# One tail load of a log-sum-exp kernel, issued as three transfers with uneven shares for the DMA engines

## The chip, the cores and the metric

The kernel runs on one core of one Trainium2 chip. The metric is the device time of one execution in microseconds (us). The median of three runs of the kernel before is 161.57 us; the three lie between 161.51 and 161.59 us. A profile was taken of one more execution. All views, line numbers and durations below come from that execution.

## The reference

The input `x` is a float32 array of 32 x 512 x 1024. For every row of 1024 numbers the reference gives the logarithm of the sum of exponentials, in its stable form:

```
max_x = np.max(x, axis=-1, keepdims=True)
max_x.squeeze(-1) + np.log(np.sum(np.exp(x - max_x), axis=-1))
```

There are 16384 such rows, so 67.11 MB are read and 0.07 MB are written.

## The kernel before, in words

**The layout.** The 16384 rows are spread over 128 partitions, 128 rows of the input to each. One such row in every partition is called a column here: 128 columns of 1024 numbers (`d`). The kernel does not subtract the maximum first. It takes the exponential and the sum directly, then tests whether all sums lie in a safe range (L276 to L294, with a small TensorE product that adds up over the partitions), and only if they do not, it computes everything again with the maximum subtracted (L302 to L345). With this input that branch is not taken.

**The loads.** `LOADS` (L22 to L28) lists 19 loads. Its first number is the load's size in columns: the first has 15.625 columns, then they shrink, the fifteenth (index 14) has 0.75 columns and the last (index 18) 0.46875. A load is one DMA of all 128 partitions (L139), so it moves one run of bytes to each partition: 3072 bytes for the fifteenth. All loads are issued in order on SyncE's queue (SP). They land in a ring of 48 columns per partition (`ring`), and `load` waits (L136) until the work that used the same place of the ring is done. Each load has a semaphore of its own, `landed[i]`, that stands at 16 when the whole load has landed.

**The work on a load.** ScalarE (ACT) waits for `landed[i]` (L186) and takes the exponential in place (L227). Then the letters of the load's plan say how the sums over the columns are made: `R` is one VectorE (DVE) reduction (L238), `G` lets GpSimd (POOL) add the two halves first (L233) and DVE reduce what is left (L157), `T` lets DVE add the two halves of one column with the sum as a by-product (L165). Loads 9 to 16 (counted from 0) have `T` columns, 16 adds with the one of load 17. Load 17 (`a`) holds the first part of the last column and is summed by DVE; load 18 (`b`) holds its last 480 numbers, which ACT exponentiates and sums itself (L222).

**The end.** `HELD` is 15: before the add of load 15, DVE also waits until load 16 has landed (L244, L245). An early store of 112 finished columns is issued on SP after load 18 (L261). When DVE's adds are done, ACT takes the logarithm of the last 16 columns (L265, then L267, which needs ACT's own sum of load 18), copies that sum (L270), and SP issues the last store (L272). Beside that DVE makes the range test's two sums (L276, L280), PE adds them up in three products (L286, L288, L290; the third one needs the copy of L270), DVE compares (L294), and ACT and DVE read the answer and branch (L297, L302). SP ends the program when both stores have landed.

**Names that the prediction uses.** A load is called by its index: load 14 is the fifteenth. `done_before` is the position of a load in the input, `here` its position in the ring.

Of the kernel before, what the change touches and what calls it, by code (L numbers as in the profile page):

```python
# [11 lines left out]
B = 16  # L12

HELD = 15

# [36 lines left out]
def kernel(  # L54
# [5 lines left out]
    nc = tc.nc  # L60
# [4 lines left out]
    P = nc.NUM_PARTITIONS  # L65
# [19 lines left out]
    def source(e0, size):  # L85
        assert e0 >= W * d or e0 + size <= W * d
        return x_rest[:, e0 - W * d : e0 - W * d + size] if e0 >= W * d else x_rows[:, e0 : e0 + size]
# [9 lines left out]
    def sbuf(name, cols, dtype=fp32, rows=P):  # L97
        return nc.alloc_sbuf_tensor(name, [rows, cols], dtype).ap()

    ring = sbuf("ring", RING * d)  # L100
# [14 lines left out]
    landed = [nc.alloc_semaphore(f"landed{i}") for i in range(len(loads))]  # L115
    act = Counted(nc, nc.scalar, "act")
# [16 lines left out]
    def load(i, here, done_before, size):  # L133
        for a, b, who, at in users:
            if a < here + size and b > here:
                sp.wait(who, at)  # L136
        assert not any(p0 < here + size and p0 + s * d > here for _, p0, s, _ in folded)
        users[:] = [u for u in users if not (u[0] < here + size and u[1] > here)]
        return nc.sync.dma_start(  # L139
            out=ring[:, here : here + size], in_=source(done_before, size)  # L140
        ).then_inc(landed[i], 16)

    c = 0
    p = 0
    here = 0
    done_before = 0
# [6 lines left out]
    def sum_folded():  # L153
        for c0, p0, s, at in folded:
            dve.wait(pool, at)
            half = ring[:, p0 : p0 + s * d].rearrange("p (c d) -> p c d", d=d)[:, :, 0:H]
            at = dve.did(nc.vector.reduce_sum(out=sumexp[:, c0 : c0 + s], in_=half, axis=AX.X))  # L157
            users.append((p0, p0 + s * d, dve, at))
            summed.append((c0, c0 + s, at))
        folded.clear()  # L160

    def add_halves(v, col):
        h = v.shape[-1] // 2
        lo = v[:, 0:h]
        return dve.did(nc.vector.scalar_tensor_tensor(  # L165
            out=lo, in0=lo, scalar=1.0, in1=v[:, h : 2 * h],
            op0=ALU.mult, op1=ALU.add, accum_out=sumexp[:, col : col + 1],
        ))

    def check_early(c):  # L170
        dve.wait(act, summed_by_act)
        dve.wait(dve, dve.n)
        for op, col in ((ALU.min, LEAST), (ALU.add, TOTAL)):
            dve.did(nc.vector.tensor_reduce(  # L174
                out=sumexp[:, col : col + 1], in_=sumexp[:, 0:c], op=op, axis=AX.X
            ))

    for i, (size, parts) in enumerate(loads):
        if here + size > RING * d:
            assert here == p  # L180
            p = here = 0
        dma = load(i, here, done_before, size)
        first_load = first_load or dma.ins
        end = here + size
        done_before += size
        act.wait(landed[i], 16)  # L186
        for k, part in enumerate(parts):
            if part[0][0] == "H":
                sum_folded()
                continue  # L190
            if part[0][0] == "C":
                assert not folded
                checked = c
                check_early(c)
                continue
            if part[0][0] == "L":
                assert c >= W
                assert dve.seen[act.sem.num] >= summed_by_act
                act.wait(dve, max(at for c0, _, at in summed if c0 < W))
                ln_early = act.did(nc.scalar.activation(  # L200
                    out=res[:, 0:W], in_=sumexp[:, 0:W], func=AF.Ln
                ))
                continue
            if part[0][0] == "A":
                assert here == p
                for _ in range(part[0][1]):
                    v = ring[:, p : p + d]
                    summed_by_act = act.did(nc.scalar.activation(
                        out=v, in_=v, func=AF.Exp, accum_out=sumexp[:, c : c + 1]
                    ))  # L210
                    users.append((p, p + d, act, summed_by_act))
                    by_act += 1
                    c += 1
                    p += d
                    here += d
                continue
            rows = sum(s for how, s in part if how in "RTG")
            more = any(q[0][0] not in "HLC" for q in parts[k + 1 :])
            upto = p + rows * d if more else end
            v = ring[:, here:upto]  # L220
            if part[-1][0] == "b":
                last = act.did(nc.scalar.activation(  # L222
                    out=v, in_=v, func=AF.Exp, accum_out=rest
                ))
                here = upto
                continue
            at = act.did(nc.scalar.activation(out=v, in_=v, func=AF.Exp))  # L227
            here = upto
            for how, s in part:
                rows = ring[:, p : p + s * d].rearrange("p (c d) -> p c d", d=d)  # L230
                if how == "G":
                    pool.wait(act, at)
                    folded.append((c, p, s, pool.did(nc.gpsimd.tensor_tensor(  # L233
                        out=rows[:, :, 0:H], in0=rows[:, :, 0:H], in1=rows[:, :, H:d], op=ALU.add,
                    ))))
                elif how == "R":
                    dve.wait(act, at)
                    users.append((p, p + s * d, dve, dve.did(nc.vector.reduce_sum(  # L238
                        out=sumexp[:, c : c + s], in_=rows, axis=AX.X
                    ))))  # L240
                    summed.append((c, c + s, dve.n))
                elif how == "T":
                    if i == HELD:
                        nc.vector.wait_ge(landed[i + 1], 16)  # L244
                        nc.vector.nop(nofuse=True)  # L245
                    dve.wait(act, at)
                    for r in range(s):
                        n_sums = add_halves(rows[:, r, :], c + r)
                        users.append((p + r * d, p + (r + 1) * d, dve, n_sums))
                        summed.append((c + r, c + r + 1, n_sums))  # L250
                elif how == "a":
                    dve.wait(act, at)
                    summed.append((LAST, NC, add_halves(ring[:, p:upto], LAST)))
                    s = 0
                c += s
                p += s * d
        assert here == end
# [10 lines left out]
        out=res[:, LAST:NC], in_=rest, func=AF.Ln, bias=sumexp[:, LAST:NC]  # L268
# [8 lines left out]
        out=clamped[:, 0 : LEAST + 1 - checked], in0=sumexp[:, checked : LEAST + 1], scalar=LOW,  # L277
# [3 lines left out]
        out=total, in_=sumexp[:, checked : TOTAL + 1], axis=AX.X  # L281
# [20 lines left out]
    with nc.If(all_fine < 1):  # L302
# [5 lines left out]
        for c0 in range(0, NC, RING):  # L308
# [6 lines left out]
            for c1, c2 in ((c0, edge), (edge, c0 + s)):  # L315
                if c1 == c2:
                    continue
                nc.scalar.dma_start(
                    out=ring[:, (c1 - c0) * d : (c2 - c0) * d],
                    in_=source(c1 * d, (c2 - c1) * d),  # L320
# [4 lines left out]
                out=neg, in_=v, op=ALU.max, axis=AX.X, negate=True  # L325
# [3 lines left out]
                out=v, in0=v, in1=neg[:, :, None].to_broadcast([P, s, d])  # L329
# [5 lines left out]
                out=sumexp[:, c0 : c0 + s], in_=v, axis=AX.X  # L335
# [70 lines left out]
```

## Time and profile before

| What | Value |
|---|---|
| median of 3 runs | 161.57 us (161.51 to 161.59) |
| the profiled execution's own time | 161.52 us |
| its span, first to last instruction | 160.2 us |
| DVE busy | 116.2 us (73%) |
| ACT busy | 114.6 us (72%) |
| POOL busy | 33.3 us (21%) |
| PE busy | 0.4 us |
| bytes moved by DMA | 67.18 MB, mean 419 GB/s over the span |

The span is 1.3 us shorter than the execution's own time; what lies around it is not in the trace. An engine's busy time is a mean over stages with different limits: early in the run ACT waits for loads, at the end the engines work back to back. The rows of a timeline give the start, the duration, the engine and line, the operation and the shapes. Instructions of one engine overlap by some hundredths of a microsecond, so a start may lie a little ahead of the end of the instruction before. The rows on DMA issues give a transfer's size and the time from its issue to its landing, so issue plus that time is the landing.

### The profile page before, as it was taken

The numbers are of one execution on the slowest core, as the hardware profiler recorded it, in microseconds if no ns is written. First come the engines' busy times: TensorE is split into PE (matmuls) and PEld (weight loads), VectorE is DVE, ScalarE is ACT, GpSimd is POOL, SyncE is SP. The second block draws the span as 40 slices with busy tenths as digits, with TensorE's granted clock in tenths as the row PEclk, the third lists the DMA queues.
The fourth block names the chain that finished last, engine by engine and source line by source line (L and its number), as shares of the span: only waits on it lengthen the run. The fifth ranks groups of instructions, "written<-read, shape, count | busy, mean of one in ns | idle before, by whom it ended". The sixth has DMA issues, their size and how long they took to land.

```text
span 160.2 us, 183 instructions
## 1 busy us (share of the span) xinstructions
PE 0.4 (0%) x6; PEld 0.3 (0%) x6; DVE 116.2 (73%) x56; ACT 114.6 (72%) x32; POOL 33.3 (21%) x14
## 2 busy tenths in 40 slices
PE   0000000000000000000000000000000000000001
PEld 0000000000000000000000000000000000000000
DVE  0000000029997599999999699929999999999996
ACT  3000069970999429992799349965998999899996
POOL 0000000000000000000000000980580589996000
DMA  8998999699599699996999999997999999999993
GB/s 272 495 511 368 400 514 482 289 514 513 256 512 512 272 479 478 478 463 268 453 467 467 467 430 430 430 430 332 499 395 448 437 417 389 443 412 423 417 409 105
DMA packets 3025, 67.18 MB, mean 419 GB/s; under 512 B 592, under 2 KB 720, under 8 KB 1488
## 3 DMA queue, kind: packets, MB, share of 16 engines
q1 hardware_dynamic: 3024, 67.18, 97.9%
q14 instruction: 1, 0.01, 0.0%
HBM read 67.11 MB, written 0.07 MB: 419 GB/s over the span
## 4 chain that ended last, share of the span: by engine, by line
DMA 53%; DVE 21%; ACT 19%; POOL 5%; issue 0%; PE 0%; SPq 0%
DMA ring<-in_x_dram 53%; ACT ring L227 19%; DVE sumexp L238 15%; POOL ring L233 5%; DVE ring L165 3%; DVE sumexp L157 2%; SPq L139 0%; DVE clamped L276 0%; PE count L286 0%; ACT res L200 0%; DVE fine L294 0%; PE count L290 0%; PE count L288 0%
## 5 line engine op out<-in xcount | busy, mean ns | idle before, releaser
L227 ACT ACTIVATE ring<-ring 128x16000 f32<-128x16000 f32 (+24 forms) x25 | 112.2, 4546 | 42.7 <-DMA ring<-in_x_dram 42.7
L238 DVE TENSOR_REDUCE sumexp<-ring 128x9 f32<-128x9216 f32 (+7 forms) x10 | 89.8, 8999 | 39.1 <-ACT ring L227 39.1
L233 POOL TENSOR_TENSOR ring<-ring 128x2048 f32<-128x2048 f32 (+5 forms) x8 | 33.0, 4133 | 112.2 <-ACT ring L227 112.1
L157 DVE TENSOR_REDUCE sumexp<-ring 128x4 f32<-128x2048 f32 (+5 forms) x8 | 16.5, 2079 | 3.4 <-POOL ring L233 3.4
L165 DVE SCALAR_TENSOR_TENSOR ring<-ring 128x512 f32<-128x512 f32 (+1 forms) x16 | 9.8, 672 | 0.1
L126 ACT ACT_TABLE_LOAD x1 | 1.3, 1283 | 1.4 <-PEq L63 1.4
L165 DVE DVE_READ_ACCUMULATOR ring<-ring 128x1 f32 x16 | 1.3, 83 | 0.0
L222 ACT ACTIVATE ring<-ring 128x480 f32<-128x480 f32 x1 | 0.6, 603 | 0.0
L286 PE MATMUL count<-far,bad 128*1 128x1 f32 x2 | 0.2, 164 | 158.6 <-DVE clamped L276 158.6
L174 DVE TENSOR_REDUCE sumexp<-sumexp 128x1 f32<-128x106 f32 x2 | 0.4, 258 | 0.0
L294 DVE TENSOR_SCALAR fine<-count 1x1 int32<-1x1 f32 x1 | 0.1, 147 | 0.4 <-PE count L290 0.4
L286 PEld LDWEIGHTS count<-far,bad 128*1 128x1 f32 x2 | 0.1, 80 | 158.6 <-DVE clamped L276 158.6
L127 POOL MEMSET ones<- 128x1 f32 x1 | 0.1, 98 | 1.0 <-POOLq L63 1.0
L200 ACT ACTIVATE res<-sumexp 128x112 f32<-128x112 f32 x1 | 0.3, 279 | 0.0
L267 ACT ACTIVATE res<-rest,sumexp 128x1 f32<-128x1 f32 x1 | 0.2, 244 | 0.0
L265 ACT ACTIVATE res<-sumexp 128x15 f32<-128x15 f32 x1 | 0.2, 216 | 0.0
L276 DVE SCALAR_TENSOR_TENSOR clamped<-sumexp 128x23 f32<-128x23 f32 x1 | 0.2, 183 | 0.0
L288 PE MATMUL count<-total,ones 128*1 128x1 f32 x2 | 0.2, 164 | 0.0
L290 PE MATMUL count<-sumexp,ones 128*1 128x1 f32 x2 | 0.2, 164 | 0.0
L280 DVE TENSOR_REDUCE total<-sumexp 128x1 f32<-128x24 f32 x1 | 0.2, 175 | 0.0
L222 ACT ACTIVATION_READ_ACCUMULATOR ring<-ring 128x1 f32 x1 | 0.2, 153 | 0.0
L270 ACT COPY sumexp<-rest 128x1 f32<-128x1 f32 x1 | 0.1, 150 | 0.0
(8 smaller groups left out, 0.8 us busy)
## 6 DMA issues: line engine op xcount, KB each, us to landing
ring<-in_x_dram SPq DMA_DIRECT2D x1, 8048.0 KB, 38.8
ring<-in_x_dram SPq DMA_DIRECT2D x1, 8016.0 KB, 57.4
ring<-in_x_dram SPq DMA_DIRECT2D x1, 8000.0 KB, 21.3
ring<-in_x_dram SPq DMA_DIRECT2D x1, 7472.0 KB, 25.8
ring<-in_x_dram SPq DMA_DIRECT2D x1, 7312.0 KB, 23.0
ring<-in_x_dram SPq DMA_DIRECT2D x1, 6720.0 KB, 21.6
ring<-in_x_dram SPq DMA_DIRECT2D x1, 5200.0 KB, 17.6
ring<-in_x_dram SPq DMA_DIRECT2D x1, 3584.0 KB, 19.1
```

The lines of the kernel that those rows point to most:

```text
L126: nc.scalar.preload_act_table_set("natural_log_exp_and_others")
L157: at = dve.did(nc.vector.reduce_sum(out=sumexp[:, c0 : c0 + s], in_=half, axis=AX.X))
L165: return dve.did(nc.vector.scalar_tensor_tensor(out=lo, in0=lo, scalar=1.0, in1=v[:, h : 2 * h], op0=ALU.mult, op1=ALU.add, accum_out=sume ...
L174: dve.did(nc.vector.tensor_reduce(out=sumexp[:, col : col + 1], in_=sumexp[:, 0:c], op=op, axis=AX.X))
L200: ln_early = act.did(nc.scalar.activation(out=res[:, 0:W], in_=sumexp[:, 0:W], func=AF.Ln))
L222: last = act.did(nc.scalar.activation(out=v, in_=v, func=AF.Exp, accum_out=rest))
L227: at = act.did(nc.scalar.activation(out=v, in_=v, func=AF.Exp))
L233: folded.append((c, p, s, pool.did(nc.gpsimd.tensor_tensor(out=rows[:, :, 0:H], in0=rows[:, :, 0:H], in1=rows[:, :, H:d], op=ALU.add,))))
L238: users.append((p, p + s * d, dve, dve.did(nc.vector.reduce_sum(out=sumexp[:, c : c + s], in_=rows, axis=AX.X))))
L265: act.did(nc.scalar.activation(out=res[:, W:LAST], in_=sumexp[:, W:LAST], func=AF.Ln))
L267: ln_last = act.did(nc.scalar.activation(out=res[:, LAST:NC], in_=rest, func=AF.Ln, bias=sumexp[:, LAST:NC]))
L286: pe.did(nc.tensor.matmul(count, lhsT=bad, rhs=far, start=True, stop=False))
```

## The change

The fifteenth load, index 14, is issued as three transfers: partitions 0 to 111, 112 to 119 and 120 to 127. Each moves the same columns as before, 3072 bytes for each partition, from the same place in the input to the same place in the ring. All three count on the semaphore of load 14, and ACT waits for 48 on it instead of 16. The other 18 loads are issued as before. The words that describe the change say that the lower eight DMA engines then move nine of this load's packets and the other eight engines seven.

```diff
+UNEVEN = 14
+SHARES = (0, 112, 120, 128)
...
-        return nc.sync.dma_start(
-            out=ring[:, here : here + size], in_=source(done_before, size)
-        ).then_inc(landed[i], 16)
+        shares = SHARES if i == UNEVEN else (0, P)
+        for p0, p1 in zip(shares, shares[1:]):
+            dma = nc.sync.dma_start(
+                out=ring[p0:p1, here : here + size], in_=source(done_before, size)[p0:p1]
+            ).then_inc(landed[i], 16)
+        return dma
...
-        act.wait(landed[i], 16)
+        act.wait(landed[i], 16 * (len(SHARES) - 1) if i == UNEVEN else 16)
```

## The prediction, made before the changed kernel ran

> **What bounds the kernel now.** I read the page first, for the totals, and then the chain of waits in order of time, for the stage that the change touches.
>
> ```profile
> span 160.2 us, 183 instructions
> q1 hardware_dynamic: 3024, 67.18, 97.9%
> DMA 53%; DVE 21%; ACT 19%; POOL 5%; issue 0%; PE 0%; SPq 0%
> ```
>
> The DMA engines have work for 97.9% of the span, and the chain that ended last is DMA for 53% of it. Load 14 comes in the last 8 us, so that share says little about it. The chain's last pieces do:
>
> ```profile
> 119.57 23.79 DMA ring<-in_x_dram
> 143.36 0.02 issue
> 143.38 6.75 ACT ring L227 x2
> 150.13 0.18 ACT res L200
> 150.32 3.74 ACT ring L227 x2
> 154.06 0.02 issue
> 154.09 2.36 DVE ring L165 x7
> 156.44 0.15 issue
> 156.60 1.74 DVE ring L165 x7
> 158.33 0.02 issue
> ```
>
> The last transfer on the chain is load 9, which lands at 119.57 + 23.79 = 143.36. From there ACT works through its exponentials, and from 154.09 DVE's adds follow one another. No later load is on the chain. The question is how much room loads 14 to 18 have, so I put landings beside the starts of ACT. The timeline of SP gives the issues of loads 14 to 18, and the DMA view their sizes and times to landing:
>
> ```profile
> 132.86 0.43 SPq L139 DMA_DIRECT2D ring<-in_x_dram  x1
> 133.33 0.47 SPq L139 DMA_DIRECT2D ring<-in_x_dram  x1
> 133.84 0.45 SPq L139 DMA_DIRECT2D ring<-in_x_dram  x1
> 134.33 4.72 SPq L139 DMA_DIRECT2D ring<-in_x_dram  x1
> 139.10 3.74 SPq L139 DMA_DIRECT2D ring<-in_x_dram  x1
> ring<-in_x_dram SPq DMA_DIRECT2D x1, 384.0 KB, 21.9
> ring<-in_x_dram SPq DMA_DIRECT2D x1, 336.0 KB, 22.3
> ring<-in_x_dram SPq DMA_DIRECT2D x1, 320.0 KB, 22.6
> ring<-in_x_dram SPq DMA_DIRECT2D x1, 272.0 KB, 22.7
> ring<-in_x_dram SPq DMA_DIRECT2D x1, 240.0 KB, 18.6
> ```
>
> ACT's timeline gives when each of them was taken up and when the logarithm begins; the last row is SP's and is the store behind it:
>
> ```profile
> 155.12 0.83 ACT L227 ACTIVATE ring<-ring 128x768 f32<-128x768 f32 x1
> 155.85 0.75 ACT L227 ACTIVATE ring<-ring 128x672 f32<-128x672 f32 x1
> 156.51 0.72 ACT L227 ACTIVATE ring<-ring 128x640 f32<-128x640 f32 x1
> 157.13 0.64 ACT L227 ACTIVATE ring<-ring 128x544 f32<-128x544 f32 x1
> 157.72 0.60 ACT L222 ACTIVATE ring<-ring 128x480 f32<-128x480 f32 x1
> 158.35 0.22 ACT L265 ACTIVATE res<-sumexp 128x15 f32<-128x15 f32 x1
> 158.75 0.34 SPq L272 DMA_DIRECT2D out_dram<-res  x1
> ```
>
> Issue plus time to landing: load 14 lands at 132.86 + 21.9 = 154.8 and is taken up at 155.12; load 15 at 155.6 for 155.85; load 16 at 156.4 for 156.51; load 17 at 157.0 for 157.13; load 18 at 139.10 + 18.6 = 157.70 for 157.72. The **room** shrinks from 0.36 us to 0.02. For load 18 ACT itself would have been ready a little earlier: neighbours overlap by 0.09 us (156.51 + 0.72 - 157.13 = 0.10, 155.85 + 0.75 - 156.51 = 0.09), so after 157.13 + 0.64 = 157.77 it could have begun at 157.68. Load 18 holds ACT up by 0.04 us and no other late load holds it at all.
>
> **What an earlier landing can give.** Of these 0.04 us nothing need arrive: L265 begins at 158.35, just behind the end of DVE's last add in the chain (158.33), and DVE's adds do not hang on load 18. So an earlier landing of loads 14 to 18 gives between 0 and 0.04 us; I take 0, because the chain ends in DVE.
>
> **What a later landing costs.** A delay D of loads 14 to 18 is eaten by the room of loads 14 to 16 as long as D is under some 0.1, but at load 18 it arrives almost whole: L222 starts D later, and with it L267, the copy L270 (which the last PE product waits for) and the store L272. So the cost is about D.
>
> **The change part by part.** The price of one packet comes first. Between the landings of loads 9 (143.36) and 18 (157.70) lie loads 10 to 18. Four more sizes complete the list:
>
> ```profile
> ring<-in_x_dram SPq DMA_DIRECT2D x1, 1584.0 KB, 24.8
> ring<-in_x_dram SPq DMA_DIRECT2D x1, 1232.0 KB, 27.4
> ring<-in_x_dram SPq DMA_DIRECT2D x1, 896.0 KB, 20.2
> ring<-in_x_dram SPq DMA_DIRECT2D x1, 640.0 KB, 21.4
> ```
>
> They sum to 4352 KB, with loads 14 to 18 (1552 KB) to 5904 KB, in 14.34 us: 412 KB/us, 25.7 KB/us for one of 16 engines. A packet of load 14 is 384 / 128 = 3 KB and takes its engine 3 / 25.7 = **0.117 us**. Eight packets to each engine become nine for half of the engines and seven for the other half: half of the engines reach load 15 0.117 us later, half 0.117 us earlier, and since all later packets queue behind, this shift stays until load 18.
>
> Two more completions fall on the engines that serve the small transfers. No row shows one alone. Load 18 takes 157.70 - 157.03 = 0.67 us after load 17, and its 240 / 16 = 15 KB an engine need 15 / 25.7 = 0.58, so all that is fixed in a load (eight packets and one completion) is at most 0.09 us, and one ninth of it 0.01. Two completions cost between 0 and 0.18 us; I take 0.02, the ninth twice, because packets follow each other without a gap. A lower engine is then 0.117 + 0.02 = 0.14 us later, an upper one 0.117 earlier.
>
> **Which engines end last** decides the sign. The table by stretches shows the engines running out of packets behind load 18 (the last column but one is the DMA share; the small early store, 56 KB, still fills in):
>
> ```profile
> 157.10:157.20 0.10, 0.00 (x0) 0.00 (x0) 0.10 (x1) 0.10 (x2) 0.00 (x0) 1.00 0.89 267
> 157.20:157.30 0.10, 0.00 (x0) 0.00 (x0) 0.10 (x3) 0.10 (x2) 0.00 (x0) 1.00 0.43 128
> 157.30:157.40 0.10, 0.00 (x0) 0.00 (x0) 0.10 (x3) 0.10 (x1) 0.00 (x0) 1.00 0.23 58
> 157.40:157.50 0.10, 0.00 (x0) 0.00 (x0) 0.10 (x1) 0.10 (x1) 0.00 (x0) 1.00 0.12 31
> 157.50:157.60 0.10, 0.00 (x0) 0.00 (x0) 0.10 (x1) 0.10 (x1) 0.00 (x0) 1.00 0.01 0
> ```
>
> 0.89 x 16 = 14 engines are busy, then 7, 4, 2 and none: the engines end over some 0.4 us, and two of them trail by about 0.1 us, one packet's time. No view names them. If both are upper engines, loads 15 to 18 land up to 0.12 us earlier, worth 0. If one or both are lower engines, loads land 0.14 later, worth +0.14 us. By mere counting both are upper in (8/16) x (7/15), about a quarter; so I take **+0.14**. The Trainium skill, "DMA: Bandwidth & Descriptors", section "Latency and other measured facts", says that DMA engines 7 and 15 are usually slower in traces, with a cause that it ties to transfers issued by GpSimd. Two trailing engines fit its count; one of that pair would be a lower engine, which also gives +0.14, while without such a pair the sum stays open between 0 and +0.14.
>
> **The issues.** SP issues two transfers more, 2 x 0.45 = 0.9 us. Loads 15 to 18 queue behind them, and so does the early store. The issues of loads 17 and 18 already last 4.72 and 3.74 us; nothing shown ends them, so SP seems to wait for room in the DMA queue. Load 18's issue is over at 142.84, its data moves in the last 0.7 us ahead of 157.70. Even if two more transfers ahead of it cost two loads' waiting, until load 11 has landed (1232 KB above, issued in the row below), it would be issued 7 us early:
>
> ```profile
> 122.72 0.44 SPq L139 DMA_DIRECT2D ring<-in_x_dram  x1
> ```
>
> 122.72 + 27.4 = 150.1. That cover hides the 0.9 us entirely; the cost is 0. No wait instruction is added; ACT's wait counts to 48 instead of 16, at no cost.
>
> **Sum.** 161.52 (the profiled execution: a span of 160.2 and 1.3 around it) + 0.14 = 161.66. That execution lies 0.05 below the median of the runs, so the forecast is **161.71 us**, +0.09%. Its own range, packets at their usual pace, is 161.50 to 161.85: the 0.04 gain below, both completions a little dearer above.
>
> **Rival 1, slower: the small transfers share a way into SBUF.** Every transfer in this trace spreads over all 128 partitions, so no row shows eight engines writing to eight neighbouring partitions. 25.7 KB/us an engine may be the pace of the engine or of the place it writes to. If each place serves 8 of 128 partitions, with neighbours together, the eight packets of a small transfer queue at one, two or four places. I take two, between one and four. There four packets follow each other: 4 x 0.117 = 0.47 us a transfer, 0.94 for both, and a lower engine needs 7 + 8 = 15 packet times instead of 8, D = 0.82. If the late engines are upper ones, some 0.2 of this falls into the spread. That gives +0.6 to +0.82: 162.2 to 162.4, middle 162.3. At one place D is (7 + 16 - 8) x 0.117 = 1.76 (163.3), at four 3 x 0.117 = 0.35 (161.9). The transfer of 112 may suffer too, since seven partitions an engine no longer match places of eight; twice its 7 x 0.117 would add up to 0.82. It decides from D = 0.32, three packet times. For it speaks that 16 equal paces fit either reading; against it that a burst of two packets an engine, 6 KB, may be absorbed on the way, and that the profile has no sign of such a queue. The Trainium skill, "SBUF — State Buffer", section "Door 1: The DMA port swizzle", states such a mapping: four neighbouring partitions lie on one port, and it gives 27.6 GB/s to partitions 0 to 3 against 104 to 0 to 15. By that rule partitions 112 to 119 reach two ports, the case of 162.3; no trace here shows it.
>
> **Rival 2: both trailing engines are upper ones**, and landings come earlier. It gives 161.53 to 161.57 for the reason above. Being within the noise it counts with the forecast.
>
> **Rival 3: the change does not do what it says.** If the small transfers spread over all engines, nothing shifts: 161.57. If one engine takes all eight packets, it has 7 + 16 instead of 8: +1.76, 163.3.
>
> **A real gain** of over 0.32 us would need ACT to begin earlier than at 143.38, which load 14 can't bring, or a large idle time behind load 14, which the rows do not have.
>
> **How the numbers follow.** 0.2% is 0.32 us, about what a measurement can tell from no change. Packets at their usual pace (with rival 2): 0.52, all of it within 0.2%. Sharing: 0.40, of which 0.38 slower and 0.02, the mildest, within 0.2%. Rival 3: 0.04, half within, half slower. Unforeseen: 0.04, half faster, half slower. So same is 0.52 + 0.02 + 0.02 = 0.56, slower 0.38 + 0.02 + 0.02 = 0.42, faster 0.02. The range reaches from 161.50 to 162.80; the harder sharing above it and a single engine are left out, at about 0.15. The likeliest case alone has 161.50 to 161.85.
>
> **What would show it.** Right: after load 14 the times to landing of loads 14 to 18 move by at most 0.15 us, L222 starts between 157.7 and 157.9, and a transfer of 8 partitions takes no longer than others. Rival 1: the DMA share drops below 0.9 in the stretch where load 14 moves, load 18 lands at 158.3 or later, ACT shows an idle gap ahead of L227's 128x768, or of the ones behind it. Rival 3: the landing moves by 0 or by over 1.5 us. The forecast is wrong if ACT waits for load 14 at all.

## The result, and the profile after

The changed kernel takes 162.14 us (median of 6 runs, 162.04 to 162.71), the kernel before beside it 161.51 us (6 runs, 161.49 to 161.59). The ratio is 1.0043, with a 95% interval from 1.0033 to 1.0054: **slower by 0.63 us**. The profiled execution of the changed kernel took 162.08 us, with a span of 160.7.

The same three lines of the page, after the change:

```profile
span 160.7 us, 185 instructions
q1 hardware_dynamic: 3040, 67.18, 97.8%
DMA 51%; DVE 31%; ACT 11%; POOL 4%; SPq 1%; issue 0%; PE 0%
```

The two new instructions are SP's issues, and the packets grew by 16: they are small ones, for the bytes are the same 67.18 MB. Nothing on the page says where 0.63 us went; the chain does. Its pieces from the issue of load 13 on, after the change (start, duration, what; the short `issue` pieces and what follows the last row are left out):

```profile
132.60 0.43 SPq L145
133.08 0.45 SPq L145
133.58 0.44 SPq L145
134.06 21.48 DMA ring<-in_x_dram
155.56 0.85 ACT ring L234
156.44 0.58 DVE ring L172
157.06 1.77 DVE ring L172 x7
158.85 0.20 DVE clamped L283 x2
```

Before, the last transfer on the chain was load 9. Now it is the third part of load 14, issued at 134.06 and landed at 155.54, where all of load 14 had landed at 154.8 before. ACT's timeline (L234 is the former L227, L229 the former L222) shows the wait in brackets, and how the late loads are taken up; below it the issue and landing of load 18:

```profile
155.56 0.84 ACT L234 ACTIVATE ring<-ring 128x768 f32<-128x768 f32 x1 [0.20 <-DMA ring<-in_x_dram]
157.67 0.66 ACT L234 ACTIVATE ring<-ring 128x544 f32<-128x544 f32 x1
158.31 0.60 ACT L229 ACTIVATE ring<-ring 128x480 f32<-128x480 f32 x1
138.79 4.08 SPq L145 DMA_DIRECT2D ring<-in_x_dram  x1
ring<-in_x_dram SPq DMA_DIRECT2D x1, 240.0 KB, 19.5
```

ACT stands idle for 0.20 us ahead of load 14, and load 18 lands at 138.79 + 19.5 = 158.29 instead of 157.70. L229 begins 158.31 - 157.72 = 0.59 us later than before. The other late path is the one on the chain: DVE waits for the exponential of load 14 and starts its add 0.46 us later than before (156.44 instead of 155.98):

```profile
156.44 0.69 DVE L172 SCALAR_TENSOR_TENSOR ring<-ring 128x512 f32<-128x512 f32 x1 [0.28 <-ACT ring L234]
155.98 0.69 DVE L165 SCALAR_TENSOR_TENSOR ring<-ring 128x512 f32<-128x512 f32 x1
```

The first row is after the change, the second before. From there DVE's adds follow one another, and the range test begins at 158.85 instead of 158.36, 0.49 later. The two paths meet in the last product on PE, which starts 0.55 us later than before (159.37 instead of 158.82). All loads from 14 on land late, and that is the loss. The issues are not it: load 18's is over at 138.79 + 4.08 = 142.87, against 142.84 before.

The view that shows the cause is the table by stretches, of 0.6 us each. The last two columns are the share of time for which the DMA engines had a packet in hand, and the GB/s that they moved. Before:

```profile
153.60:154.20 0.60, 0.00 (x0) 0.00 (x0) 0.54 (x3) 0.60 (x2) 0.00 (x0) 1.00 1.02 408
154.20:154.80 0.60, 0.00 (x0) 0.00 (x0) 0.60 (x3) 0.60 (x1) 0.00 (x0) 1.00 1.03 413
154.80:155.40 0.60, 0.00 (x0) 0.00 (x0) 0.60 (x3) 0.60 (x2) 0.00 (x0) 1.00 1.05 418
```

After:

```profile
153.60:154.20 0.60, 0.00 (x0) 0.00 (x0) 0.59 (x2) 0.60 (x2) 0.00 (x0) 1.00 1.02 360
154.20:154.80 0.60, 0.00 (x0) 0.00 (x0) 0.57 (x1) 0.60 (x1) 0.00 (x0) 1.00 1.11 244
154.80:155.40 0.60, 0.00 (x0) 0.00 (x0) 0.60 (x3) 0.56 (x1) 0.00 (x0) 1.00 0.98 320
155.40:156.00 0.60, 0.00 (x0) 0.00 (x0) 0.60 (x3) 0.44 (x1) 0.00 (x0) 1.00 1.03 405
```

The engines are as busy as before, but they move 244 GB/s where they moved 413. A packet takes longer, no engine is out of work. The trace's records of single packets say it directly: before, every packet of load 15 (2688 bytes) took 0.107 us; after the change they took 0.158 on average and up to 0.233, and those of load 14 (3072 bytes) 0.128 on average instead of 0.121. So most of the loss falls on the load behind the split one. The missing bytes are (48 + 169 + 98) GB/s x 0.6 us = 189 KB, which at 410 GB/s is 0.46 us of all engines. A full DMA share is no sign of a full rate; the column beside it must be read too.

### The profile page after: what moved, and what is told of

Read it like the earlier page. It is cut to its first block, busy times and chain, and to the rows that moved or that the text cites. A ratio compares the mean times of both kernels' runs of the same rounds, so it can differ in the third digit from the quotient of the medians.

```text
span 160.7 us, 185 instructions
## 1 busy us (share of the span) xinstructions
PE 0.5 (0%) x6; PEld 0.3 (0%) x6; DVE 116.2 (72%) x56; ACT 114.8 (71%) x32; POOL 33.3 (21%) x14
## 2 busy tenths in 40 slices
DMA packets 3041, 67.18 MB, mean 418 GB/s; under 512 B 608, under 2 KB 736, under 8 KB 1504
## 3 DMA queue, kind: packets, MB, share of 16 engines
q1 hardware_dynamic: 3040, 67.18, 97.8%
## 4 chain that ended last, share of the span: by engine, by line
DMA 51%; DVE 31%; ACT 11%; POOL 4%; SPq 1%; issue 0%; PE 0%
DMA ring<-in_x_dram 51%; DVE sumexp L245 27%; ACT ring L234 11%; POOL ring L240 4%; DVE sumexp L164 2%; DVE ring L172 1%; SPq L145 1%; DVE clamped L283 0%; PE count L297 0%; PE count L293 0%; DVE fine L301 0%; PE count L295 0%; SPq L54 0%
## 5 line engine op out<-in xcount | busy, mean ns | idle before, releaser
L234 ACT ACTIVATE ring<-ring 128x16000 f32<-128x16000 f32 (+24 forms) x25 | 112.4, 4548 | 43.1 <-DMA ring<-in_x_dram 43.1
L229 ACT ACTIVATE ring<-ring 128x480 f32<-128x480 f32 x1 | 0.6, 602 | 0.0
L229 ACT ACTIVATION_READ_ACCUMULATOR ring<-ring 128x1 f32 x1 | 0.2, 154 | 0.0
```

Of the source, the lines that this page charges most:

```text
L229: last = act.did(nc.scalar.activation(out=v, in_=v, func=AF.Exp, accum_out=rest))
```

## The experiments

**The theory** after this reading: the packets of load 14 meet on the way into SBUF, because neighbouring partitions are served at a common place (rival 1 of the prediction, called the sharing theory in the expectations). The 0.59 us that the expectations start from is the delay of load 18's landing. **The rivals**: a fixed price for each transfer; the uneven shares themselves; neighbouring input rows that meet in HBM. The diffs below are extracts: counts on semaphores and the allocation of new tiles are left out.

### Three transfers by columns

Load 14 is cut by columns instead of partitions:

```diff
+        cuts = (0, size // 3, 2 * size // 3, size) if i == 14 else (0, size)
+        for c0, c1 in zip(cuts, cuts[1:]):
+            dma = nc.sync.dma_start(
+                out=ring[:, here + c0 : here + c1], in_=source(done_before + c0, c1 - c0)
+            ).then_inc(landed[i], 16)
```

> Load 14 as three transfers of all 128 partitions, 256 columns each (1 KB a packet); every engine gets the same. Sharing theory (eight neighbouring partitions queue at few places in SBUF): all partitions are spread, so load 18 lands within 0.1 us of before (157.70) and the time is 161.5 to 161.6. Rival, a fixed price for each transfer (0.59 us for the change's two more transfers, 0.3 each): load 18 lands near 158.3, time near 162.1.

Measured: 161.58 us against 161.58, ratio 1.0002 (0.9992 to 1.0011). Every packet of loads 15 to 18 took as long in the trace as before. Two more transfers, with their issues and with completions on every engine, cost nothing that can be measured here. The fixed price falls.

### No uneven shares

```diff
-SHARES = (0, 112, 120, 128)
+SHARES = (0, 112, 128)
```

> Load 14 as two transfers, 112 and 16 partitions, eight packets to every engine, so no uneven shares. Sharing theory: sixteen neighbours at four places, four packets each, 7 + 4 = 11 packet times instead of 8, at most 3 x 0.117 = 0.35 us, and about 0.25 by the ratio that the change showed (0.59 of 0.82): time 161.7 to 161.9. Rival, uneven shares: nothing is left of the loss, 161.5. Rival, a price for each transfer: +0.3, 161.8.

Measured: 162.04 us, ratio 1.0029 (1.0017 to 1.0042), a loss of 0.46 us. It is above the range that I gave the sharing theory. The engines have equal shares here, so the uneven shares cannot carry the loss; and 0.46 is more than the 16 partitions alone should cost by that theory (0.35 at most). The transfer of 112 had to be looked at too.

### The two small transfers alone, near and spaced

Load 14 stays whole. Two transfers of 8 partitions more follow it, into a tile `scratch` that nothing reads. The one run takes neighbours, the other every fourth partition:

```diff
+            for part in (slice(112, 120), slice(120, 128)):      # neighbours
+            for part in (slice(0, 32, 4), slice(32, 64, 4)):     # spaced
+                nc.sync.dma_start(
+                    out=scratch[part], in_=source(done_before, size)[part]
+                ).then_inc(spare, 16)
```

> The kernel before, load 14 whole, with two more transfers of 8 partitions behind it, partitions 112 to 119 and 120 to 127, into a scratch tile that nothing reads. Sharing theory: 8 + 8 = 16 packet times for a lower engine, +0.94 us at most, about 0.7 by the ratio of the change: time 162.1 to 162.4. Rival, a price for each transfer: 0.6 and two packets (0.23), 162.1 to 162.3, the same as the next run.

> As the run before, same bytes and number of transfers, but the eight partitions are every fourth one, 0, 4 to 28 and 32, 36 to 60. Sharing theory with neighbours together: each of the eight has a place of its own, so a lower engine only has two packets more, 2 x 0.117 + two completions = 0.26 at most, less if the engines that end last are upper ones: time 161.5 to 161.8. Rival, a price for each transfer: as the run before, 162.1 to 162.3.

Measured: neighbours 162.02 us, ratio 1.0024 (1.0014 to 1.0034); spaced 161.56 us, ratio 1.0000 (0.9991 to 1.0010). Same bytes, same number of transfers and engines: only which partitions go together, and with them the rows read, differ. The loss of the neighbours, 0.44 us, is below the 0.7 that I expected; that of the spaced ones is none. The table by stretches for the neighbours:

```profile
153.60:154.20 0.60, 0.00 (x0) 0.00 (x0) 0.60 (x3) 0.60 (x1) 0.00 (x0) 1.00 1.04 414
154.20:154.80 0.60, 0.00 (x0) 0.00 (x0) 0.59 (x3) 0.60 (x2) 0.00 (x0) 1.00 1.13 285
154.80:155.40 0.60, 0.00 (x0) 0.00 (x0) 0.60 (x3) 0.60 (x1) 0.00 (x0) 1.00 0.96 336
```

and for the spaced ones:

```profile
153.60:154.20 0.60, 0.00 (x0) 0.00 (x0) 0.49 (x3) 0.60 (x2) 0.00 (x0) 1.00 1.01 408
154.20:154.80 0.60, 0.00 (x0) 0.00 (x0) 0.60 (x3) 0.60 (x1) 0.00 (x0) 1.00 1.05 415
154.80:155.40 0.60, 0.00 (x0) 0.00 (x0) 0.60 (x3) 0.60 (x2) 0.00 (x0) 1.00 1.03 407
```

The same dip as in the changed kernel, 285 and 336 GB/s, comes with the neighbours and not with the spaced ones, and the packets of load 15 took 0.144 us on average with the neighbours and 0.107 each with the spaced ones. The neighbours lie in partitions 112 to 127 and the spaced ones in 0 to 60, so this pair alone doesn't tell neighbours from upper partitions; the pair with ten and six packets below bears on that.

### Which side they meet on

The neighbours again, but the source rows are the spaced ones (`in_=source(done_before, size)[rows]`, with `rows` 0, 4 to 28 and 32, 36 to 60). What lands in `scratch` is read by nothing.

> The extra transfers as in the third run, to the scratch partitions 112 to 119 and 120 to 127, but their source rows are every fourth one of the input. Sharing on SBUF's side: the loss of the third run stays, 161.9 to 162.1. Rival, neighbouring rows of the input meet in HBM: the loss goes, 161.5 to 161.6.

Measured: 162.09 us, ratio 1.0029 (1.0018 to 1.0041). The dip stays:

```profile
154.20:154.80 0.60, 0.00 (x0) 0.00 (x0) 0.60 (x1) 0.60 (x1) 0.00 (x0) 1.00 1.11 295
154.80:155.40 0.60, 0.00 (x0) 0.00 (x0) 0.60 (x3) 0.53 (x2) 0.00 (x0) 1.00 0.95 324
```

This run and the spaced one read the same rows of the input and differ in the target partitions alone. So the packets of the small transfers meet on SBUF's side, and the rival in HBM falls.

### The transfer of 112 partitions alone

Load 14 stays whole, with one more transfer into `scratch`: partitions 0 to 111 in one run, all 128 in the other.

```diff
+            for part in (slice(0, 112),):      # (slice(0, 128),) in the other run
```

> The kernel before with one more transfer behind load 14, partitions 0 to 111 into a scratch tile that nothing reads: seven packets more for every engine. If the transfer of 112 keeps its packets apart, this costs 7 x 0.117 = 0.82 us, 0.12 less than the next run: time 162.4, the next run 162.5. If seven partitions an engine meet at places of eight (sharing theory, second half), it costs more than the next run although it moves less: 162.6 to 163.2.

> As the run before with all 128 partitions: eight packets more for every engine, none meeting, +0.94 us: time 162.5, and the DMA rate stays at 400 GB/s or more through the stretch.

Measured: 112 partitions 162.77 us, ratio 1.0070 (1.0056 to 1.0083); 128 partitions 162.41 us, ratio 1.0057 (1.0044 to 1.0071). The smaller transfer has the higher median, by 0.36 us. The two intervals overlap, so the medians alone would not carry this; the rates do. (The profiled execution took 163.07 us with 112 and 162.33 with 128, so the two traces lie further apart than the medians.) With 112:

```profile
154.20:154.80 0.60, 0.00 (x0) 0.00 (x0) 0.56 (x2) 0.60 (x2) 0.00 (x0) 1.00 1.08 378
154.80:155.40 0.60, 0.00 (x0) 0.00 (x0) 0.60 (x3) 0.60 (x2) 0.00 (x0) 1.00 1.03 273
155.40:156.00 0.60, 0.00 (x0) 0.00 (x0) 0.60 (x3) 0.60 (x1) 0.00 (x0) 1.00 1.03 260
```

With 128:

```profile
154.20:154.80 0.60, 0.00 (x0) 0.00 (x0) 0.60 (x3) 0.60 (x1) 0.00 (x0) 1.00 1.05 425
154.80:155.40 0.60, 0.00 (x0) 0.00 (x0) 0.60 (x3) 0.60 (x2) 0.00 (x0) 1.00 1.04 415
155.40:156.00 0.60, 0.00 (x0) 0.00 (x0) 0.60 (x3) 0.45 (x1) 0.00 (x0) 1.00 1.01 402
```

The 112 partitions draw the rate down to 260 GB/s, the 128 do not. With 128, every packet of 3072 bytes took 0.121 us as before; with 112, 47 of the 240 took longer, 0.178 on average. That the small transfers are not needed for the dip is shown. How the 112 are dealt to the engines no view tells, and whether they too meet on SBUF's side no run tested.

The changed kernel itself shows the same. The page of the run with 112 partitions more counts 128 packets more than before (3152 against 3024), 112 for the rows and 16 small ones, as for a load on all 16 engines, so an engine's share of 112 partitions is taken as seven packets. In the changed kernel the first packet of load 14 starts at 153.00, and seven take 7 x 0.121 = 0.85 us, so up to 153.84 no packet of the small transfers can have started. Eight of the 98 packets started by then already took 0.135 to 0.160 us.

### The last sixteen dealt out otherwise

```diff
+        parts = (slice(0, 112), slice(112, 128, 2), slice(113, 128, 2)) if i == 14 else (slice(0, P),)
```

> The change with its last sixteen partitions dealt out otherwise: 112, 114 to 126 in one transfer and 113, 115 to 127 in the other; same shares, nothing left out. Sharing theory with four neighbours to a place: two packets meet instead of four, 7 + 4 = 11 packet times for a lower engine instead of 15, so a loss of at most half that of the change: 161.7 to 161.9. If most of the change's loss comes from the transfer of 112: as the change, 162.0 to 162.2.

Measured: 162.11 us, ratio 1.0033 (1.0021 to 1.0045), a loss of 0.54 us against the 0.63 of the change, with overlapping intervals. By the theory half of the meetings in the small transfers are gone; that changes little while the 112 stay, which is the second expectation.

### Ten and six packets

Load 14 as partitions 32 to 127 and four transfers of 8 partitions, counted to 80 on its semaphore:

```diff
+        parts = (slice(32, 128), slice(0, 8), slice(8, 16), slice(16, 24), slice(24, 32))       # neighbours
+        parts = (slice(32, 128), slice(0, 32, 4), slice(1, 32, 4), slice(2, 32, 4), ...)        # spaced
```

> Load 14 as partitions 32 to 127 and four transfers of 8 neighbours (0 to 7, 8 to 15, 16 to 23, 24 to 31), nothing left out: ten packets for a lower engine, six for an upper. Sharing theory: 6 + 4 x 4 = 22 packet times instead of 8, +1.6 us at most, 0.9 to 1.2 by the ratios of the change and of the extra transfers: time 162.4 to 162.8. Rival, uneven shares alone: +0.23 at most, the same as the next run.

> As the run before, the same 32 partitions in four transfers of 8 and the same ten and six packets, but each transfer takes every fourth partition (0, 4 to 28; 1, 5 to 29; and so on). Sharing theory: no two packets of a transfer meet, so only the shares count, +0.23 and the completions at most: time 161.4 to 161.8. Rival, uneven shares or a price for each transfer: as the run before.

Measured: neighbours 162.39 us, ratio 1.0046 (1.0030 to 1.0063); spaced 162.23 us, ratio 1.0043 (1.0029 to 1.0057). The neighbours are just below the 162.4 that was expected at least. The spaced run is a clear miss: it should have lost 0.2 us at most. Its rates say why:

```profile
153.60:154.20 0.60, 0.00 (x0) 0.00 (x0) 0.56 (x3) 0.37 (x1) 0.00 (x0) 1.00 1.04 280
154.20:154.80 0.60, 0.00 (x0) 0.00 (x0) 0.60 (x3) 0.60 (x1) 0.00 (x0) 1.00 1.00 285
154.80:155.40 0.60, 0.00 (x0) 0.00 (x0) 0.51 (x2) 0.60 (x1) 0.00 (x0) 1.00 1.06 420
```

The dip comes earlier than with the extra transfers behind a whole load 14 (280 GB/s from 153.60 to 154.20, where those still had 414 and 408), and it is over at 154.80. That is the head of load 14, where the transfer of 96 partitions runs. The packets confirm it: the first packet of load 14 starts at 152.96 here, and six packets an engine, the share of 96 partitions, take 6 x 0.121 = 0.73 us, so up to 153.68 no small transfer can have started. By then 21 of 72 packets had taken 0.14 to 0.22 us. So the transfer of 96 slows itself as that of 112 does. I had left this out of the expectation.

The run with neighbours has the dip for one stretch more:

```profile
153.60:154.20 0.60, 0.00 (x0) 0.00 (x0) 0.57 (x3) 0.60 (x2) 0.00 (x0) 1.00 1.03 301
154.20:154.80 0.60, 0.00 (x0) 0.00 (x0) 0.60 (x3) 0.60 (x1) 0.00 (x0) 1.00 1.05 291
154.80:155.40 0.60, 0.00 (x0) 0.00 (x0) 0.60 (x3) 0.41 (x1) 0.00 (x0) 1.00 1.03 310
```

Both runs put the same 32 partitions into small transfers, and from 154.80 the neighbours move 310 GB/s where the spaced ones move 420. This speaks for neighbours and against a slow upper part of the partitions as the cause. It rests on one trace each; the two medians are too close to tell them apart.

### A larger packet

```diff
-UNEVEN = 14
+UNEVEN = 12
```

> The change made at load 12 (7168 bytes a packet) instead of load 14 (3072), same shares. Sharing theory: the loss grows with the packet, 0.59 x 7168 / 3072 = 1.4 us (or 1.7 if a fixed part is absorbed on the way): time 162.9 to 163.2. Rival, a price for each transfer or for the uneven number of transfers: the loss is that of the change, 162.1.

Measured: 163.90 us, ratio 1.0148 (1.0131 to 1.0165), a loss of 2.28 us, more than the range that I gave the sharing theory (162.9 to 163.2). The packet is 2.33 times larger and the loss 2.28 / 0.63 = 3.6 times. A fixed price falls again, and plain proportion does too. The loss grows faster than the packet, as when a first part of it is absorbed; from two sizes, at two places of the tail, no law follows.

### What an earlier landing is worth

Load 14 brings 7/8 of its columns, POOL sets the other 96 to zero long before, and ACT and DVE keep all their work:

```diff
+        got = size if i != 14 else size * 7 // 8
+            cleared[:] = [pool.did(nc.gpsimd.memset(ring[:, here + got : here + size], 0.0))]
-            out=ring[:, here : here + size], in_=source(done_before, size)
+            out=ring[:, here : here + got], in_=source(done_before, got)
```

> What an earlier landing is worth. Load 14 brings only 672 of its 768 columns, the other 96 are set to zero by POOL long before (so their exponentials are 1), and all work of ACT and DVE stays. Every engine is freed 1/8 of the load earlier, 0.12 us, for loads 14 to 18. By the prediction's step (0 to 0.04 us, taken as 0): time 161.5 to 161.6, load 18 lands at 157.6 and ACT starts L222 at 157.68. Rival, the late landing of load 18 holds the end: 161.45.

Measured: 161.77 us, ratio 1.0011 (1.0002 to 1.0020): not faster, but 0.2 us slower. ACT's timeline:

```profile
157.20 0.64 ACT L235 ACTIVATE ring<-ring 128x544 f32<-128x544 f32 x1
157.75 0.59 ACT L230 ACTIVATE ring<-ring 128x480 f32<-128x480 f32 x1
158.42 0.21 ACT L273 ACTIVATE res<-sumexp 128x15 f32<-128x15 f32 x1
```

The exponential of load 18 begins at 157.75, 0.09 ahead of the end of its neighbour (157.84), as back-to-back instructions do; ACT no longer waits for the load, which landed 0.08 us earlier than before (157.62 instead of 157.70), and nothing is won, because the logarithm still follows at 158.42. The extra 0.2 us is left open. ACT's late rows begin 0.07 us later than before in this trace (load 17 at 157.20 instead of 157.13), and this execution took 161.82 us with a span of 160.3, so 1.5 us lie around the span instead of 1.3; the trace does not show that part. Against such a shift a gain of 0 to 0.04 us could not be seen.

## Why the prediction was wrong in its forecast, and right in a rival

**The forecast** was 161.71 us, the time came out at 162.14. It is inside the range (161.50 to 162.80) and on the side to which 0.42 was given, but by the mechanism of rival 1, not by that of the forecast: the forecast's own range, 161.50 to 161.85, is missed by 0.29 us, and only the part of the range added for rival 1 holds the result. Two of the signs that the prediction had named say the same: ACT waited for load 14 (0.20 us), and L229, the former L222, started at 158.31 instead of 157.7 to 157.9.

**What bounds the end: held.** The prediction said that a delay of load 18 arrives almost whole. Load 18 landed 0.59 later, L229 began 0.59 later, and the medians differ by 0.63. The room of load 14 did not absorb its own delay, for that was larger than the 0.1 us that the prediction allowed for. The run with 128 partitions more gives a check of the packet's price: 8 x 0.117 = 0.94 was worked out, 162.41 - 161.57 = 0.84 measured.

**What an earlier landing gives: held as far as the runs tell.** 0 to 0.04 us, taken as 0; the run with less data was no faster, though its open 0.2 us would hide so small a gain. By the rows, ACT and DVE leave no more to be won, so the change could hardly have gained even if its shares had evened out when the engines end.

**The issues and the completions: held, and smaller than bounded.** Three column transfers cost nothing measurable; the 0 to 0.18 us for two completions is at its lower end.

**The step that failed** is the price of the packets: "packets at their usual pace", with D = 0.14. In the changed kernel they do not keep it: 244 GB/s against 413 in the middle stretch, and 0.158 us for a packet of load 15 instead of 0.107. Load 18 came 0.59 us later, not 0.14. The argument against rival 1, that a burst of 6 KB an engine "may be absorbed on the way", was a guess, and two runs of the pair near and spaced refuted it. The prediction's rule for taking it (no such row in the trace) was weak: a trace in which every load covers 128 partitions cannot show the case.

**Which engines end last** was not decided. The spaced run puts two packets more on eight engines, 2 x 0.117 + 0.02 = 0.25 if these were the last ones, and the median did not move; ACT took up load 18 there at 157.82, 0.10 later:

```profile
157.82 0.60 ACT L230 ACTIVATE ring<-ring 128x480 f32<-128x480 f32 x1
```

So the +0.14 for one packet was too dear, as far as this run tells, and the counting of engines that gave it settled nothing. Rival 2, both trailing engines among the upper ones, is neither shown nor refuted.

**Rival 1: the right mechanism for the small transfers, and a sum that fits in part by luck.** Its price was 0.6 to 0.82 us for the small transfers, with up to 0.82 more for the 112. The measured loss, 0.63, is at the lower end of the first; the time, 162.14, is just below the 162.2 to 162.4 because the kernel before ran at 161.51 this time. The runs order this otherwise: the two small transfers alone cost 0.44 us, 112 partitions cost 0.36 more than 128 although they move less, and together in the change they cost 0.63. The parts do not add up to the whole, and why is open. That the 112 slow the stream is shown, that they do it by the same mechanism is not. The sign named for this rival, a DMA share below 0.9, did not come: the share was 1.11 and 0.98 in the slow stretches, and only the GB/s fell. The Trainium skill, "SBUF — State Buffer", section "Door 1: The DMA port swizzle", has four neighbouring partitions on one port and every fourth one on another. The runs agree: 1.0024 for neighbours, 1.0000 for every fourth partition.

**Rival 3**, a change that does not do what it says, is left with little. The page counts 16 packets more with two more transfers, and also 16 more in the run whose one more transfer has 16 partitions (3040 in both): eight small packets for each transfer of 8 partitions, as if eight engines served it. An engine with 16 packets more would have cost 1.76 us by the prediction's price, and equal shares lose nearly as much as the change does.

## What to carry to other kernels

Balance the DMA engines by where packets land as well as by how many there are: here a transfer of 112 partitions, or two of eight neighbours, brought the stream down to about two thirds of its rate while the engines looked fully busy. Read GB/s beside the DMA share, by stretches as short as the transfer. Before evening out a queue, look whether the last landing holds anything: here the engines behind it were back to back, and there was at most 0.04 us to win.

## What was not expected of the hardware

A single transfer of 112 partitions slowed the stream to 260 GB/s, where one of 128 kept 402 to 425. The loads behind were held up too: the packets of load 15 took 0.153 us on average in that run, where they took 0.107 before. And the loss grew 3.6 times for a packet 2.33 times larger.
